# The down product of a feed-forward layer by one level of Strassen's scheme

## The chip, the cores and the metric

One core of a Trainium2 chip. Its engines are TensorE (PE, matmuls; PEld is its loading of the stationary operand), VectorE (DVE), ScalarE (ACT), GpSimd (POOL) and SyncE (SP, which here issues DMAs). The metric is the device time of one execution in microseconds, lower is better; the median of three runs is compared.

## The reference, cut to what matters

The program is one encoder block on 512 tokens of width 1024: a gated-delta branch and a short convolution, mixed, a layer norm, and then a feed-forward part, which is all that this change concerns:

```python
x = layer_norm(DEEPNORM_ALPHA * x + mixed @ w_out, ln1_g, ln1_b)
h = square(relu(x @ w_up + b_up))                    # 512 x 4096
x = layer_norm(DEEPNORM_ALPHA * x + h @ w_down + b_down, ln2_g, ln2_b)
```

`w_down` is 4096 x 1024, so the last product has 512 x 4096 x 1024 multiplications. Everything is float32.

## The kernel before

A float32 operand goes into TensorE as two parts, a higher part (`wh`, `hh`, rounded by a ScalarE copy) and a lower part (`wl`, `hl`, the VectorE difference of the operand and its higher part). One product of two tiles is then three matmuls: high x high, high x low, low x high. The helper `split` (lines 105 and 106) makes the two parts, `split_w` (lines 124 and 120) the same for the weights of `proj`.

After the first layer norm the product with `w_up` runs over 32 chunks of 128 columns. Each takes 24 matmuls of 128x512 in `proj` (lines 158 to 160); then `up_end` applies the ReLU on ScalarE (line 951) and squares on GpSimd (line 953), and the result `hf32[f]` (128 hidden units x 512 tokens, float32) stays in the slab under the tags A, A, D and C, eight chunks each.

The product with `w_down` is `tok_product` with `KF` = 32 chunks of rows. All eight banks of PSUM hold one accumulator each: four tiles of 128 tokens by two halves of 512 columns. Each chunk loads 512 KB of `w_down` over SP's queue (`load_w2`, line 890), splits it, splits `hf32[k]`, and for each of the eight accumulators runs `down`: three matmuls whose stationary operand is a 128x128 piece of the activations and whose moving operand is 512 columns of weights (line 899). The last four chunks (`tail`) are kept back and run tile after tile, so that a tile's end, `finish2`, runs beside the matmuls of the next tile. `finish2` adds the accumulators to `xs[t]`, the residual (line 993), takes the row statistics (`bn_stats`, line 873, and lines 877 to 880), and normalizes: the columns from `cut` on go through ScalarE (line 1002) and GpSimd (lines 1003 and 1004), the others through VectorE (lines 1008 and 1009). Then the tile is stored.

Weights pass through two rings: `raw` (three tiles in `wpool`) and `w2h`/`w2l` (four each in `ffn`). The split activations use the ring `wh`/`wl` of `wpool` (two each), which also holds the weights of the up product. Two pools matter for space: `late` holds the split input `x1` of the up product and is released at the very end.

Outside of regions marked `tc.manual_schedule` the framework orders instructions of an engine itself, by their dependences; inside such a region each engine listed keeps the order in which the program is written.

Of the kernel before, what the change touches and what calls it, by code (L numbers as in the profile page):

```python
# [61 lines left out]
def kernel(  # L62
# [912 lines left out]
    hpair = {}  # L975

    def h_split(k):
        if k % 2 == 0:
# [1 line left out]
        a, b = hpair[k - k % 2]  # L980
        a, b = a[:, k % 2, :], b[:, k % 2, :]
        split(a, b, hf32[k])
        return a, b

    def finish2(t, accs):
# [1 line left out]
        n = 2
        w = D // n
        part, end = row_stats(y, n, f"2_{t}")
        for j in range(n):  # L990
            js = slice(j * w, (j + 1) * w)
            o = j * w % NT
            tt(out=y[:, js], in0=y[:, js], in1=accs[j * w // NT][:, o:o + w], op=ALU.add)
# [74 lines left out]
```

## Time and profile before

| | |
|---|---|
| median of three runs | 1059.67 us (1056.95 to 1060.29) |
| the profiled execution | 1056.44 us, its span 1054.7 us |
| TensorE busy | 1025.2 us, 97% of the span |
| VectorE, ScalarE, GpSimd busy | 532.5, 452.6, 286.2 us |
| granted TensorE clock, mean | 0.991 |
| up product in `proj` | to 870.5 us |
| down product | 870.5 to 1044.9 us |
| HBM | 97.27 MB read |

Busy time of TensorE is modelled from pipelined instructions, so a matmul's row shows a longer duration than the distance between two of them. The rate comes from a stretch divided by its matmuls.

### The profile page before, as it was taken

How to read it: one execution, taken by the hardware profiler on the slowest of the kernel's cores; microseconds unless marked ns; L12 is line 12 of the kernel's file. 1: busy time of each engine (PE TensorE's matmuls, PEld its weight loads, DVE VectorE, ACT ScalarE, POOL GpSimd, SP SyncE). 2: the span in 40 equal slices, each digit the busy share in tenths (PEclk: the TensorE clock that was granted, in tenths of full speed). 3: DMA queues.
4: the chain of work that ended last, by engine and by line, in shares of the span. 5: the costliest groups of instructions: out<-in, count | busy, mean ns of one | idle time of the engine just before them, and what ended most of it. 6: DMA issues, size and time to landing. Idle time of an engine off the chain costs nothing.

```text
span 1054.7 us, 16601 instructions
## 1 busy us (share of the span) xinstructions
PE 1025.2 (97%) x6611; PEld 850.6 (81%) x6611; DVE 532.5 (50%) x923; ACT 452.6 (43%) x820; POOL 286.2 (27%) x527
## 2 busy tenths in 40 slices
PE   8898999999999999999999999989999999999996
PEld 5686888787888888888888888788888888888885
DVE  6675676767677775442322264761222243333346
ACT  5662556575757574353434232323333243232221
POOL 1051525252525346311130021263222220000005
PEclk9988999999999999999999999999999999999998
DMA  6413242323332222222335334222333342333312
GB/s 200 141 48 92 68 115 60 108 50 107 79 101 82 83 66 69 73 85 91 100 105 216 100 105 134 81 81 84 97 100 100 100 141 80 100 100 100 100 40 80
DMA packets 57094, 101.80 MB, mean 97 GB/s; under 512 B 30712, under 2 KB 32440, under 8 KB 57016
## 3 DMA queue, kind: packets, MB, share of 16 engines
q1 hardware_dynamic: 56584, 100.07, 31.2%
q8 instruction: 52, 0.85, 0.3%
q10 hardware_dynamic: 432, 0.66, 0.2%
q14 instruction: 26, 0.21, 0.1%
HBM read 97.27 MB, written 3.44 MB: 95 GB/s over the span
## 4 chain that ended last, share of the span: by engine, by line
PE 84%; DVE 6%; DMA 3%; POOL 3%; ACT 1%; issue 1%; SPq 1%; POOLq 0%; DVEq 0%; ACTq 0%
PE accd L899 16%; PE ps_in L158 11%; PE ps_in L160 10%; PE ps_in L159 10%; PE ps_up L159 5%; PE ps_up L160 5%; PE ps_up L158 5%; PE acco L899 3%; POOL X L550 2%; PE psup L946 1%; PE ps_osc L158 1%; PE ps_osc L160 1%; PE ps_osc L159 1%; PE ps_ogd L159 1%; PE ps_ogd L160 1%; PE ps_ogd L158 1%
## 5 line engine op out<-in xcount | busy, mean ns | idle before, releaser
L158 PE MATMUL ps_in<-xh,wh_in 128*128 128x512 f32 x576 | 238.5, 414 | 1.2 <-ACT wh_in L124 1.0
L160 PE MATMUL ps_in<-xh,wl_in 128*128 128x512 f32 x576 | 226.2, 393 | 1.8 <-DVE wl_in L120 1.8
L159 PE MATMUL ps_in<-xl,wh_in 128*128 128x512 f32 x576 | 225.8, 392 | 0.0
L120 DVE TENSOR_TENSOR wl_in<-raw_in,wh_in 128x1024 fp32r<-128x1024 f32 x70 | 97.4, 1391 | 86.9 <-ACT wh_in L124 86.3
L160 PEld LDWEIGHTS ps_in<-xh,wl_in 128*128 128x128 f32 x576 | 108.6, 189 | 26.8 <-DVE wl_in L120 2.7
L158 PEld LDWEIGHTS ps_in<-xh,wh_in 128*128 128x128 f32 x576 | 109.0, 189 | 21.8 <-ACT wh_in L124 2.0
L159 PEld LDWEIGHTS ps_in<-xl,wh_in 128*128 128x128 f32 x576 | 109.2, 190 | 17.7
L124 ACT ACTIVATE wh_in<-raw_in 128x1024 fp32r<-128x1024 f32 x70 | 73.9, 1056 | 71.0 <-PE ps_in L159 52.9
L899 PE MATMUL accd<-wh_down,hh 128*128 128x512 f32 x256 | 99.6, 390 | 0.0
L899 PE MATMUL accd<-wh_down,hl 128*128 128x512 f32 x256 | 99.4, 389 | 0.0
L899 PE MATMUL accd<-wl_down,hh 128*128 128x512 f32 x256 | 99.4, 389 | 0.0
L120 DVE TENSOR_TENSOR wl_up<-raw_up,wh_up 128x1024 fp32r<-128x1024 f32 x30 | 36.8, 1225 | 121.5 <-ACT wh_up L124 121.5
L158 PE MATMUL ps_up<-x1h,wh_up 128*128 128x512 f32 x224 | 87.1, 389 | 0.0
L159 PE MATMUL ps_up<-x1l,wh_up 128*128 128x512 f32 x224 | 87.1, 389 | 0.0
L160 PE MATMUL ps_up<-x1h,wl_up 128*128 128x512 f32 x224 | 87.1, 389 | 0.0
L953 POOL TENSOR_TENSOR hf<-r 128x512 f32<-128x512 f32 x32 | 46.3, 1447 | 118.6 <-ACT r L951 118.6
L124 ACT ACTIVATE wh_up<-raw_up 128x1024 fp32r<-128x1024 f32 x30 | 31.8, 1060 | 106.3 <-PE ps_up L159 98.7
L106 DVE TENSOR_TENSOR wl_down<-raw_down,wh_down 128x1024 fp32r<-128x1024 f32 x32 | 40.1, 1253 | 50.1 <-ACT wh_down L105 48.7
L899 PEld LDWEIGHTS accd<-wh_down,hh 128*128 128x128 f32 x256 | 48.0, 188 | 10.4 <-ACT wh_down L105 0.4
L899 PEld LDWEIGHTS accd<-wh_down,hl 128*128 128x128 f32 x256 | 48.0, 188 | 10.1
L899 PEld LDWEIGHTS accd<-wl_down,hh 128*128 128x128 f32 x256 | 48.0, 188 | 9.9
L105 ACT ACTIVATE wh_down<-raw_down 128x1024 fp32r<-128x1024 f32 x32 | 33.7, 1053 | 50.8 <-PE accd L899 50.2
(268 smaller groups left out, 1853.9 us busy)
## 6 DMA issues: line engine op xcount, KB each, us to landing
raw_in<-in_w_in SPq DMA_DIRECT2D x70, 512.0 KB, 3.6
raw_up<-in_w_up SPq DMA_DIRECT2D x32, 512.0 KB, 3.6
raw_down<-in_w_down SPq DMA_DIRECT2D x32, 512.0 KB, 3.5
grow<-gcd SPq DMA_DIRECT2D x8, 512.0 KB, 4.8
raw_osc<-in_w_o_sc SPq DMA_DIRECT2D x8, 512.0 KB, 3.6
raw_ogd<-in_w_o_gdn SPq DMA_DIRECT2D x8, 512.0 KB, 3.6
raw_out<-in_w_out SPq DMA_DIRECT2D x8, 512.0 KB, 3.6
xr<-in_xT SPq DMA_DIRECT2D x8, 256.0 KB, 5.0
```

Source lines behind the costliest of these rows:

```text
L105: act(out=hi, in_=src, func=AF.Copy)
L106: (lo_eng or nc.vector).tensor_tensor(out=lo, in0=src, in1=hi.bitcast(F32), op=ALU.subtract)
L120: (nc.gpsimd if pool else nc.vector).tensor_tensor(out=wl, in0=raw, in1=wh.bitcast(F32), op=ALU.subtract)
L124: act(out=wh, in_=raw, func=AF.Copy)
L158: nc.tensor.matmul(acc, wh[:, c], mh[k], start=(k == 0), stop=False)
L159: nc.tensor.matmul(acc, wh[:, c], ml[k], start=False, stop=False)
L160: nc.tensor.matmul(acc, wl[:, c], mh[k], start=False, stop=(k == KT - 1))
L550: sub(out=X[:, 0:r, k + 1:16], in0=X[:, 0:r, k + 1:16], in1=t[:, :, m], op=ALU.add)
L899: nc.tensor.matmul(acc[:, o], a[:, ts_], b[:, hs], start=start and j == 0, stop=stop and j == 2, skip_group_check=True)
L946: nc.tensor.matmul(acc[:, ts_], a[:, c], b[k][:, ts_], start=(k == 0 and t2 == 0 and j == 0), stop=(k == KT - 1 and t2 == 1 and j == 2), s ...
L953: nc.gpsimd.tensor_tensor(out=hfl, in0=r, in1=r, op=ALU.mult)
```

## The change

C = H W is computed by blocks. A pair of row chunks 2c and 2c+1 of `w_down` gives a 2 x 2 matrix of blocks on the right (rows 2c, rows 2c+1; left and right 512 columns), and the two chunks of the activations with the tokens 0 to 255 (`lo_t`) and 256 to 511 (`hi_t`) one on the left. One level of Strassen's scheme in Winograd's form takes seven products of blocks in place of eight, with sums and differences of blocks as operands. A product of blocks is, for each of two tiles of 128 tokens, three matmuls of 128x512 as before.

Seven accumulators and the added results do not fit into eight banks together, so the work runs in two passes over the 16 pairs, 32 steps in all. **Pass A** (steps 0 to 15) makes four products into aX, aY, aZ, aV (two banks each); at its last step (`left_over`) aX is copied to `e1` by ScalarE, and aY, aZ and aV are added to parts of `xs` by VectorE, six adds. **Pass B** (steps 16 to 31) goes on adding three products into aX, aZ and aY. It loads the weights again, 512 KB and 256 KB a step.

Sums of weights: in pass A GpSimd makes three differences of 128x512 in place in the raw weights (`sums_a`); in pass B one of 128x512, and one of 128x256 of the activations. Sums of activations in pass A: three of 128x256 on VectorE (two in `sums_a`, one in `parts_a`). All of these come before the splitting of their results by `split_d` and `split_h`. After pass A GpSimd also adds `e1` to parts of `xs`, one of six such adds in each of six steps.

Order: the loop is in a `manual_schedule` for all four engines. At step n it issues the loads of step n+3, the splits of step n+1, the sums of step n+2, and the matmuls of step n. Steps 0 and 1 are prepared, and step 2 is loaded, ahead of the loop. Raw weights go through a ring of seven tiles: three of `wpool`, two of `ffn`, two of the new pool `dn`, which takes the place of `late`, now released before the down product. The last five steps (`TAIL_B`) are all prepared after the loop's last matmuls have been issued, and then run for one half of the accumulators after the other: aY, aX, aZ for tokens of q = 0, then for q = 1, with the ends of two token tiles (`finish2`, now a generator) in between.

```diff
+ORDER = (2, 0, 3, 1)
+CUT = (0, NT, NT // 2, 3 * D // 4)
+TAIL_B = 5
+HOME_W, HOME_H = {11: "A", 15: "A"}, {11: "A", 15: "D"}
...
-    def h_split(k):
-        if k % 2 == 0:
-            hpair[k] = (wpool.tile([P, 2, NT], F32R, tag="wh", name=f"hh{k}"), wpool.tile([P, 2, NT], F32R, tag="wl", name=f"hl{k}"))
...
+    def load_d(k, lo, n, i):
+        j = i % 7
+        pool, tag, bufs = (wpool, "raw", 3) if j < 3 else (ffn, "rawx", 2) if j < 5 else (dn, "raw", 2)
+        raw = pool.tile([P, D], F32, tag=tag, name=f"raw_down{i}", bufs=bufs)
+        nc.sync.dma_start(out=raw[:, :n], in_=w_down[k][:, lo:lo + n])
+        return raw
+
+    def split_d(raw, n, i, home=None):
...
+        pool, tag = (ffn, "w2") if home is None else (home, "w1")
+        wh = pool.tile([P, n], F32R, tag=tag + "h", name=f"wh_down{i}", bufs=4)
+        wl = pool.tile([P, n], F32R, tag=tag + "l", name=f"wl_down{i}", bufs=4)
+        split(wh, wl, raw[:, :n])
+        return [(wh[:, j * NT:(j + 1) * NT], wl[:, j * NT:(j + 1) * NT]) for j in range(n // NT)]
+
+    late.release()
+    dn = tc.alloc_tile_pool(name="dn", bufs=1)
...
+    def split_h(k, parts, home=None):
...
+        pool, w, bufs = (dn, 3, 1) if i == 2 else (wpool, 4, 2)
+        sh_ = pool.tile([P, w, HT], F32R, tag="wh", name=f"hh{k}", bufs=bufs)
+        sl_ = pool.tile([P, w, HT], F32R, tag="wl", name=f"hl{k}", bufs=bufs)
+        o = 0
+        for src, w in parts:
+            split(flat(sh_[:, o:o + w]), flat(sl_[:, o:o + w]), src)
+            o += w
...
+    def sums_a(c, r0, r1):
+        sub = nc.gpsimd.tensor_tensor
+        sub(out=r0[:, right], in0=r0[:, right], in1=r0[:, left], op=ALU.subtract)
+        sub(out=r1[:, right], in0=r1[:, right], in1=r0[:, right], op=ALU.subtract)
+        sub(out=r1[:, left], in0=r1[:, left], in1=r1[:, right], op=ALU.subtract)
+        x, y = hf32[2 * c], hf32[2 * c + 1]
+        s = ffn.tile([P, 2, HT], F32, tag="S", name=f"sa{c}", bufs=2)
+        tt(out=s[:, 0], in0=x[:, hi_t], in1=y[:, hi_t], op=ALU.add)
+        tt(out=s[:, 1], in0=s[:, 0], in1=x[:, lo_t], op=ALU.subtract)
+        return r0, r1, s
+
+    def parts_a(c, r0, r1, s):
+        x, y = hf32[2 * c], hf32[2 * c + 1]
+        b11, t1 = split_d(r0, D, 2 * c)
+        a11, a22, s1, s2 = split_h(c, ((x[:, lo_t], 1), (y[:, hi_t], 1), (flat(s), 2)))
+        t4, t2 = split_d(r1, D, 2 * c + 1)
+        tt(out=y[:, hi_t], in0=y[:, lo_t], in1=s[:, 1], op=ALU.subtract)
+        return (a11, b11), (s2, t2), (s1, t1), (a22, t4)
+
+    def loads_b(c):
+        i = KF + 2 * c
+        return load_d(2 * c + 1, 0, D, i), load_d(2 * c, NT, NT, i + 1)
+
+    def sums_b(c, r0, r1):
+        nc.gpsimd.tensor_tensor(out=r1[:, :NT], in0=r0[:, NT:], in1=r1[:, :NT], op=ALU.subtract)
+        x = hf32[2 * c]
+        nc.gpsimd.tensor_tensor(out=x[:, lo_t], in0=x[:, lo_t], in1=x[:, hi_t], op=ALU.subtract)
+        return r0, r1
...
+    def weights_b(c, r0):
+        return split_d(r0, D, KF + 2 * c, HOME_W.get(c))
+
+    def sums_parts_b(c, r1):
+        a = split_h(KT + KF + c, ((hf32[2 * c + 1], 2), (hf32[2 * c][:, lo_t], 1)), HOME_H.get(c))
+        return a + split_d(r1, NT, KF + 2 * c + 1, HOME_W.get(c, dn))
+
+    def strassen(acc, a, b, q, start, stop):
+        qs = slice(q * P, (q + 1) * P)
+        for j, (l_, r_) in enumerate(((a[0], b[0]), (a[0], b[1]), (a[1], b[0]))):
+            nc.tensor.matmul(acc, l_[:, qs], r_, start=start and j == 0, stop=stop and j == 2, skip_group_check=True)
...
-    tok_product(KF, "d", h_split, lambda k: load_w2(w_down[k], f"down{k}"), finish2)
...
+    aX, aY, aZ, aV = ([ps(b, f"down{b}{i}_{q}") for q, b in enumerate(bs)] for i, bs in
+                  enumerate((("s", "s"), ("l", "o"), ("m", "g"), ("m", "g"))))
...
+    with tc.manual_schedule(engines=MANUAL):
+        for n in range(2 * KP - TAIL_B):
+            ahead(n + 3, 0)
+            if n:
+                ahead(n + 1, 2)
+            ahead(n + 2, 1)
...
+                for q in range(2):
+                    strassen(acc[q], a, b, q, n == 0, n == KP - 1 and acc is aV)
+                    if n == KP - 1:
+                        left_over(j, acc, q)
+            if n > KP and adds:
+                q, t, hs = adds.pop(0)
+                y = xs[t][:, hs]
+                nc.gpsimd.tensor_tensor(out=y, in0=y, in1=e1[q], op=ALU.add)
...
+        for i, n in enumerate(ends):
+            if i:
+                ahead(n, 1)
+            if i == 3:
+                weights(ends[0])
+            sums[n] = sums_parts_b(n - KP, got[n][1])
+        for n in ends[1:]:
+            weights(n)
+    last = list(zip(*(got[n] for n in range(2 * KP - TAIL_B, 2 * KP))))
+    with tc.manual_schedule(engines={mybir.EngineType.DVE, mybir.EngineType.PE}):
+        for q in (ORDER[1], ORDER[3]):
+            f1, f0 = finish2(q + 2), finish2(q)
+            next(f1), next(f0)
+            for acc, ab_ in ((aY, last[1]), (aX, last[0]), (aZ, last[2])):
+                for a, b in ab_:
+                    strassen(acc[q], a, b, q, False, b is ab_[-1][1])
+                if acc is aY:
+                    f1.send(acc[q]), f1.send(acc[q]), next(f1)
+                else:
+                    f0.send(acc[q])
+            next(f0)
...
```

## Rows read from the trace of the kernel before

**Rows 1.** The page: busy time by engine, and the chain that ended last.

```profile
PE 1025.2 (97%) x6611; PEld 850.6 (81%) x6611; DVE 532.5 (50%) x923; ACT 452.6 (43%) x820; POOL 286.2 (27%) x527
...
PE 84%; DVE 6%; DMA 3%; POOL 3%; ACT 1%; issue 1%; SPq 1%; POOLq 0%; DVEq 0%; ACTq 0%
PE accd L899 16%; PE ps_in L158 11%; PE ps_in L160 10%; PE ps_in L159 10%; PE ps_up L159 5%; PE ps_up L160 5%; PE ps_up L158 5%; PE acco L899 3%; POOL X L550 2%; PE psup L946 1%; PE ps_osc L158 1%; PE ps_osc L160 1%; PE ps_osc L159 1%; PE ps_ogd L159 1%; PE ps_ogd L160 1%; PE ps_ogd L158 1%
```

**Rows 2.** Busy time by stretches: the start, the down product, the tail.

```profile
core 0: us, PE busy (x) PEld busy (x) DVE busy (x) ACT busy (x) POOL busy (x), PEclk, DMA share, GB/s
0.00:10.00 10.00, 8.28 (x34) 5.98 (x34) 5.06 (x10) 6.53 (x10) 2.53 (x11) 1.00 0.80 273
...
870.50:1044.90 174.40, 174.40 (x769) 143.77 (x767) 67.98 (x81) 49.82 (x65) 10.63 (x5) 1.00 0.26 83
1044.90:1055.00 10.10, 0.04 (x1) 0.00 (x0) 5.21 (x12) 1.18 (x3) 4.18 (x4) 0.72 0.35 134
```

**Rows 3.** Groups by line and shape, from 840 us on: the down product's matmuls.

```profile
line engine op names shapes xcount | busy us, mean ns | idle before us <-releasers
L899 PE MATMUL accd<-wh_down,hh 128*128 128x512 f32 x256 | 99.6, 390 | 0.0
L899 PE MATMUL accd<-wh_down,hl 128*128 128x512 f32 x256 | 99.4, 389 | 0.0
L899 PE MATMUL accd<-wl_down,hh 128*128 128x512 f32 x256 | 99.4, 389 | 0.0
```

**Rows 4.** Groups by line and shape, several stretches: splits, squares, two-input operations.

```profile
L105 ACT ACTIVATE wh_down<-raw_down 128x1024 fp32r<-128x1024 f32 x32 | 33.7, 1053 | 50.8 <-PE accd L899 50.2 <-DMA raw_down<-in_w_down 0.6
L105 ACT ACTIVATE hh<-hf 128x512 fp32r<-128x512 f32 x32 | 18.7, 624 | 62.1 <-PE accd L899 58.2 <-PE ps_up L159 4.0
L953 POOL TENSOR_TENSOR hf<-r 128x512 f32<-128x512 f32 x7 | 9.6, 1372 | 27.6 <-ACT r L951 27.6
L120 DVE TENSOR_TENSOR wl_up<-raw_up,wh_up 128x1024 fp32r<-128x1024 f32 x5 | 6.1, 1226 | 19.1 <-ACT wh_up L124 19.1
...
L495 DVE TENSOR_TENSOR na<-pg,dec 128x256 f32<-128x256 f32 x8 | 2.8, 416 | 0.4 <-PE pg L491 0.4
...
L865 POOL TENSOR_TENSOR sga<-sga,yb 128x512 f32<-128x512 f32 x8 | 10.3, 1289 | 74.7 <-DVE sga L864 74.7
```

**Rows 5.** VectorE in order of time: start, duration, instructions one behind another.

```profile
871.08 0.69 DVE L106 TENSOR_TENSOR hl<-hf,hh 128x512 fp32r<-128x512 f32 x1 [2.15 <-ACT hh L105]
...
881.96 1.29 DVE L106 TENSOR_TENSOR hl<-hf,hh 128x512 fp32r<-128x512 f32 x2 [3.62 <-ACT hh L105]
...
401.07 1.42 DVE L495 TENSOR_TENSOR na<-pg,dec 128x256 f32<-128x256 f32 x4
```

**Rows 6.** In order of time: VectorE and GpSimd where they meet.

```profile
605.47 1.28 POOL L865 TENSOR_TENSOR sga<-sga,yb 128x512 f32<-128x512 f32 x1 [45.68 <-DVE sga L864]
605.50 2.33 DVE L120 TENSOR_TENSOR wl_ogd<-raw_ogd,wh_ogd 128x1024 fp32r<-128x1024 f32 x1 [0.18 <-ACT wh_ogd L124]
...
517.97 1.23 DVE L120 TENSOR_TENSOR wl_in<-raw_in,wh_in 128x1024 fp32r<-128x1024 f32 x1 [4.21 <-ACT wh_in L124]
...
518.50 1.84 POOL L835 TENSOR_TENSOR yb<-sgb,yb 128x512 f32<-128x512 f32 x1 [2.72 <-ACT sgb L834]
...
871.65 1.04 POOL L953 TENSOR_TENSOR hf<-r 128x512 f32<-128x512 f32 x1 [4.40 <-ACT r L951]
...
872.19 1.04 DVE L106 TENSOR_TENSOR hl<-hf,hh 128x512 fp32r<-128x512 f32 x1 [0.42 <-ACT hh L105]
```

**Rows 7.** In order of time: VectorE and GpSimd in the tail.

```profile
1041.12 2.40 POOL L1004 TENSOR_TENSOR xs<-xs,ln_b 128x1024 f32<-128x1024 f32 x1
1046.61 1.26 POOL L1004 TENSOR_TENSOR xs<-xs,ln_b 128x512 f32<-128x512 f32 x1
1050.91 0.72 POOL L1004 TENSOR_TENSOR xs<-xs,ln_b 128x256 f32<-128x256 f32 x1
...
1041.23 2.83 DVE L1008 SCALAR_TENSOR_TENSOR xs<-xs,mv,ln_g 128x512 f32<-128x512 f32 x1
...
1044.91 0.68 DVE L993 TENSOR_TENSOR xs<-xs,accd 128x512 f32<-128x512 f32 x1
1046.24 0.67 DVE L993 TENSOR_TENSOR xs<-xs,accd 128x512 f32<-128x512 f32 x1
```

**Rows 8.** DMA issues: size and median microseconds from issue to landing.

```profile
raw_down<-in_w_down SPq DMA_DIRECT2D x32, 512.0 KB, 3.5
```

**Rows 9.** TensorE's waits (in total, times, longest), and stretches as in rows 2.

```profile
PE pg L491 <- ACT qh L471: 2.3, 1, 2.3
PE pg L491 <- DVE ql L473: 2.3, 1, 2.3
...
PE px L571 <- DVE UT L564: 3.1, 1, 3.1
...
PE pt L932 <- DVE xs L926: 2.6, 2, 1.3
...
52.60:59.40 6.80, 5.30 (x22) 4.91 (x23) 6.36 (x14) 3.80 (x8) 0.36 (x1) 0.50 0.26 77
...
86.70:93.50 6.80, 6.12 (x167) 4.76 (x168) 2.75 (x12) 1.87 (x5) 0.00 (x0) 0.50 0.51 198
680.00:700.00 20.00, 17.23 (x111) 14.99 (x110) 19.89 (x23) 4.77 (x8) 14.05 (x5) 1.00 0.15 52
```

More of the change, by code (lines that the diff above doesn't have):

```diff
@@ L973 @@
     nc.sync.dma_start(out=lnc["b"], in_=ln2_b.partition_broadcast(P))
-    hpair = {}
-    def h_split(k):
-        if k % 2 == 0:
-            hpair[k] = (wpool.tile([P, 2, NT], F32R, tag="wh", name=f"hh{k}"), wpool.tile([P, 2, NT], F32R, tag="wl", name=f"hl{k}"))
[L980 to L985, printed above, removed]
-        y = xs[t]
[L987 to L993, printed above, removed]
+    def load_d(k, lo, n, i):
[4 more added lines that the diff above has]
+        return raw
@@ new lines, in split_d @@
+    def split_d(raw, n, i, home=None):
+        if isinstance(home, str):
+            ws = [[slab.tile([P, NT], F32R, tag=home, name=f"w{x}_down{i}_{j}", bufs=SLOTS[home]) for x in "hl"] for j in range(n // NT)]
+            for j, (wh, wl) in enumerate(ws):
+                split(wh, wl, raw[:, j * NT:(j + 1) * NT])
+            return [tuple(w) for w in ws]
+        pool, tag = (ffn, "w2") if home is None else (home, "w1")
[3 more added lines that the diff above has]
+        return [(wh[:, j * NT:(j + 1) * NT], wl[:, j * NT:(j + 1) * NT]) for j in range(n // NT)]
@@ new lines @@
+    late.release()
+    dn = tc.alloc_tile_pool(name="dn", bufs=1)
+    SLOTS = {"A": 16, "D": 8, "C": 8}
+    HT = NT // 2
+    lo_t, hi_t = slice(0, HT), slice(HT, NT)
+    three = [0]
+    def split_h(k, parts, home=None):
+        got = []
+        if home is not None:
+            for j, (src, w) in enumerate(parts):
+                if w == 1:
+                    t = slab.tile([P, 2, HT], F32R, tag=home, name=f"ha{k}", bufs=SLOTS[home])
+                    pair = t[:, 0:1], t[:, 1:2]
+                else:
+                    pair = [slab.tile([P, w, HT], F32R, tag=home, name=f"h{x}{k}", bufs=SLOTS[home]) for x in "hl"]
+                split(flat(pair[0]), flat(pair[1]), src)
+                got += [(pair[0][:, i], pair[1][:, i]) for i in range(w)]
+            return got
+        n = sum(w for _, w in parts)
+        i = three[0] % 3 if n == 3 else 0
+        three[0] += n == 3
+        pool, w, bufs = (dn, 3, 1) if i == 2 else (wpool, 4, 2)
[5 more added lines that the diff above has]
+            o += w
+        return [(sh_[:, j], sl_[:, j]) for j in range(o)]
@@ new lines, with flat, loads_a @@
+    left, right = slice(0, NT), slice(NT, D)
+    def flat(s):
+        return s.rearrange("p a t -> p (a t)")
+    def loads_a(c):
+        return load_d(2 * c, 0, D, 2 * c), load_d(2 * c + 1, 0, D, 2 * c + 1)
+    def sums_a(c, r0, r1):
[8 more added lines that the diff above has]
+        return r0, r1, s
@@ new lines, in sums_b, with parts_b @@
+    def sums_b(c, r0, r1):
[3 more added lines that the diff above has]
+        return r0, r1
+    def parts_b(c, r0, r1):
+        w, (a12, s4, s3, t3) = weights_b(c, r0), sums_parts_b(c, r1)
+        return (a12, w[0]), (s3, t3), (s4, w[1])
+    def weights_b(c, r0):
+        return split_d(r0, D, KF + 2 * c, HOME_W.get(c))
@@ new lines, in sums_parts_b, with finish2 @@
+    def sums_parts_b(c, r1):
[5 more added lines that the diff above has]
+            nc.tensor.matmul(acc, l_[:, qs], r_, start=start and j == 0, stop=stop and j == 2, skip_group_check=True)
+    def finish2(t):
+        y = xs[t]
+        n = ORDER.index(t)
+        part, end = row_stats(y, 2, f"2_{t}")
+        for j in range(2):
+            js = slice(j * NT, (j + 1) * NT)
+            tt(out=y[:, js], in0=y[:, js], in1=(yield), op=ALU.add)
@@ L994, in finish2 @@
             part(j)
+        yield
         mv, rs = end()
-        cut = (0, 0, NT, 3 * D // 4)[t]
+        cut = CUT[n]
         if cut < D:
@@ L1010, in finish2 @@
             (nc.sync if lo % NT else nc.scalar).dma_start(out=out[t][:, js], in_=y[:, js])
-    tok_product(KF, "d", h_split, lambda k: load_w2(w_down[k], f"down{k}"), finish2)
+        yield
+    KP = KF // 2
+    aX, aY, aZ, aV = ([ps(b, f"down{b}{i}_{q}") for q, b in enumerate(bs)] for i, bs in
+                  enumerate((("s", "s"), ("l", "o"), ("m", "g"), ("m", "g"))))
+    steps = [(loads_a, sums_a, parts_a, c) for c in range(KP)] + [(loads_b, sums_b, parts_b, c) for c in range(KP)]
+    e1, got = [None, None], {}
@@ new lines, in ahead, with left_over, weights @@
+    def ahead(n, what):
+        if n < 2 * KP:
+            c = steps[n][3]
+            got[n] = steps[n][what](c, *got.get(n, ()))
+    def left_over(n, acc, q):
+        if n == 0:
+            e1[q] = slab.tile([P, NT], F32, tag="zt", name=f"e1{q}", bufs=2)
+            act(out=e1[q], in_=acc[q], func=AF.Copy)
+        else:
+            y = xs[(q, q + 2, q + 2)[n - 1]][:, (right, right, left)[n - 1]]
+            tt(out=y, in0=y, in1=acc[q], op=ALU.add)
+    def weights(n):
+        w, (a12, s4, s3, t3) = weights_b(n - KP, got[n][0]), sums[n]
+        got[n] = (a12, w[0]), (s3, t3), (s4, w[1])
@@ new lines @@
+    adds = [(q, t, hs) for q in range(2) for t, hs in ((q + 2, left), (q + 2, right), (q, right))]
+    for n in range(2):
+        for what in range(3):
+            ahead(n, what)
+    ahead(2, 0)
+    with tc.manual_schedule(engines=MANUAL):
[4 more added lines that the diff above has]
+            ahead(n + 2, 1)
+            c = steps[n][3]
+            for j, (acc, (a, b)) in enumerate(zip((aX, aY, aZ, aV) if n < KP else (aX, aZ, aY), got[n] if n < KP else [got[n][i] for i in (0, 2, 1)])):
+                for q in range(2):
[6 more added lines that the diff above has]
+                nc.gpsimd.tensor_tensor(out=y, in0=y, in1=e1[q], op=ALU.add)
+        ends = list(range(2 * KP - TAIL_B + 1, 2 * KP))
+        for n in ends[2:]:
+            ahead(n, 0)
+        sums = {}
+        for i, n in enumerate(ends):
[6 more added lines that the diff above has]
+            weights(n)
@@ new lines @@
+    last = list(zip(*(got[n] for n in range(2 * KP - TAIL_B, 2 * KP))))
[8 more added lines that the diff above has]
+                    f1.send(acc[q]), f1.send(acc[q]), next(f1)
+                else:
+                    f0.send(acc[q])
+            next(f0)
@@ L1013 @@
     ffn.tile([P, PAD_RIGHT // 4], F32, tag="pad", name="pad_right", bufs=1)
-    late.release()
+    dn.release()
 def _layout(x, w_in, conv_qkv, a_log, dt_bias, gdn_norm_w, w_o_gdn, conv_sc, w_o_sc, w_out,
```

## The prediction

> **What bounds the kernel now.** I read the page from the top. TensorE is busy in 97% of the span and carries 84% of the chain that ended last, the down product alone 16% [rows 1]. The table by stretches then shows that from 870.5 us, where the up product ends, to 1044.9 us TensorE is never idle, at the full granted clock, while VectorE works 68 of 174.4 us, ScalarE 50 and GpSimd 11 [rows 2]. This stretch is what the change rebuilds. Its groups give the price of a matmul: 768 matmuls (three lines of 256) in 174.4 us are 0.227 us each; the 389 ns of a row are a modelled end in a pipeline [rows 3]. After the last matmul comes a tail of VectorE, ScalarE, GpSimd and one store, 9.8 us.
>
> The sum is made against the profiled execution: span 1054.7 us, 1056.4 us in all, 0.3% below the median of 1059.67 us. Some 0.3% is also what a measurement of this kernel can tell from no change.
>
> **Matmuls.** A step is one pair of row chunks. Pass A has 4 products of 2 x 3 matmuls (24, 5.45 us), pass B has 3 (18, 4.09 us); 16 steps of each are 672 matmuls in place of 768. Removed: 96 x 0.227 = 21.8 us. Were TensorE still the bound, the kernel would be that much faster. So the question is whether the operands arrive in time.
>
> **Preparation of a pass A step.** VectorE: two 128x1024 lower halves (1.226 us), one 128x512 (0.69 [rows 5]), and five 256-wide (two lower halves, the three sums `s`, `s`, `y`), for which the nearest row is 128x256 at 0.416 [rows 4]. One behind another they take less than their durations, since starts overlap: two of 512 took 1.29 us together, so 0.60 for the second; four of 256 took 1.42 us, so 0.335 each [rows 5]; by the same 0.09 us, 1.14 for 1024. VectorE alone: 2 x 1.14 + 0.60 + 5 x 0.335 = 4.56 us, which fits into 5.45. ScalarE: 2 x 1.053 + 0.624 + two of 256 at most 0.62 each, 4.0 us, fits. GpSimd: three chained subtractions of 128x512 with two different inputs, 1.29 us each undisturbed [rows 4], 3.9 us, fits too. Each engine by itself hides under TensorE.
>
> **But VectorE and GpSimd do not run beside each other here.** The lower half `wl_ogd` starts 0.03 us after GpSimd's `sga` and takes 2.33 us in place of 1.226: it ends 1.08 us after GpSimd does. The other way round GpSimd's `yb` starts half a microsecond into a lower half and takes 1.84 us in place of 1.29, ending 1.14 us after VectorE; `hl`, behind GpSimd's square, takes 1.04 in place of 0.69 [rows 6]. Whoever comes second waits for the other's instruction, and only some 0.15 us of its fixed part is hidden. The exception is VectorE's adds with one input in PSUM: `xs<-xs,accd` kept 0.67 us beside GpSimd [rows 7]. All operands of the lower halves and sums lie in SBUF, so all of them count.
>
> The two engines therefore share one account. In pass A GpSimd's three take 3 x 1.14 = 3.43 us, VectorE's eight 4.56, less 0.06 for each of the three that follow GpSimd (1.08 against 1.14): 4.38. Together **7.81 us a step, against 5.45 of TensorE**. In pass B: VectorE 1.14 + 2 x 0.60 + 0.335 less 2 x 0.06, 2.56; GpSimd one subtraction of 512 (1.14) and one of 256 (0.72 [rows 7] less 0.15, 0.57); together 4.28 against 4.09. Bounds for a pass A step: whole durations with nothing hidden, 2 x 1.226 + 0.69 + 5 x 0.416 + 3 x 1.29 = 9.1 (and 5.0 in pass B); below, GpSimd's subtractions at 0.90, as its square (1.04 undisturbed) would pay: 7.1. I take 7.81, because a 512-wide GpSimd operation with two inputs stands in the rows.
>
> The Trainium skill (SBUF — State Buffer, section Who interferes with whom) has this as an exclusive lock: a VectorE instruction with two SBUF inputs and a GpSimd instruction that reads SBUF exclude each other, and the second is blocked until the first is done. Taken as whole instructions this rule would make an estimated 9.1 us a step and some 30 us more in all than my sum; the rows agree on the lock but show 0.15 us of each instruction outside it, so I keep the lower figure.
>
> **The lookahead does not absorb this.** Only steps 0 and 1 are prepared ahead of the hand-ordered loop; buffers (two steps of weights, seven raw tiles) let the rest run some two steps in front. The up product's stretch has room for these two: per chunk of 5.45 us VectorE's one lower half takes 1.23 and GpSimd's one square 1.4 [rows 4].
>
> **The sum, from 870.5 us on.** (a) The split of step 1's activations, whose buffers are up's weights, 0.60 + 2 x 0.335 = 1.27, and the square of chunk 31, 0.90: 2.2. (b) Raw tiles 5 and 6 lie in the pool that takes the place of x1, so they load only when up is over: 3.5 us to landing [rows 8], then step 2's two last subtractions; some of that is filled with other work. Nothing to 5, I take 3.0. (c) Steps 2 to 15: 14 x 7.81 = 109.3. (d) Between the passes VectorE adds six accumulators to `xs` (0.68 each, one input in PSUM) and queues step 17's splits behind them: 0 to 4.1, I take 2.0, as GpSimd goes on meanwhile. (e) 16 x 4.28 = 68.5. (f) GpSimd's six adds of `e1`, 6 x 1.08 = 6.5. (g) When the last weight is split, TensorE still has 3 + 15 + 45 matmuls (the rest of aX, aZ, the second half): 63 x 0.227 = 14.3. Together 205.8 in place of 174.4: **+31.4**.
>
> (h) The tail. In the last tile both halves were added behind 1044.9, at 1044.91 and 1046.24, because VectorE came late: its `xs` of 1041.23 took 2.83 us beside GpSimd's 2.40 [rows 7]. Now the left half is added while aZ runs, 3.4 us earlier, which takes one add and one statistic, 1.3 us, off the path; 0 to -1.3, I take -1.3. Loads: 1 MB per 7.81 us (134 GB/s), then 0.79 MB per 4.28 us (184 GB/s), 64 issues on SP in place of 32; the first stretch moved 273 GB/s [rows 2]. I cost them at nothing; their cover is three steps of lookahead, and one late load would cost at most its 3.5 us. Sum: 1056.4 + 31.4 - 1.3 = **1086.5 us**, said as 1087.
>
> **Rivals.** *Faster: the account never fills.* If GpSimd's subtractions fitted into the gaps that VectorE leaves (waits for ScalarE, the fixed parts of its short operations), TensorE stays the bound: 1056.4 - 21.8 - 1.3 + 0 to 3 = 1033 to 1036, say 1034. For it speak the three single loads, all under 5.45, against it every pair that meets in [rows 6]. It decides by one number: everything but (c) is 96.5 us, so the change breaks even at a pass A step of (174.4 + 1.3 - 96.5) / 14 = 5.7 us. To get there from 7.81, two of three subtractions would have to cost nothing. I give it 0.19. In between, within 0.3%, lies little: 0.05.
>
> *Slower still: the clock.* In pass A TensorE would work 5.45 of 7.81 us, with waits in each step: for the second weight tile, whose lower half stands last in VectorE's order. In the kernel before, after two waits of 2.3 us near 50 us, the granted clock was 0.5 (1.2 of 2.4 GHz) from 52.6 to 59.4 us, and after a wait of 3.1 us again from 86.7 for 6.8 us; with two waits of 1.3 us between 680 and 700 us it stayed at 1.00 [rows 9]. Mine are 2.4 us a step in all, longer where GpSimd runs ahead and takes every second turn. At half the clock a step needs 10.9 us of TensorE, so each fall of 6.8 us costs up to 3.4 us. Four falls give up to 13.6: 1087 to 1101. Chance 0.16.
>
> **How the numbers follow.** The forecast has 0.60, the clock 0.16, faster 0.19, the same 0.05. The forecast's own range is 1072 (7.1 a step, 14 x 0.7 = 10, and nothing for b and d, 5) to 1100 (half of what the whole durations would add, 14 x 1.3 + 16 x 0.75 = 30). With the clock on top the upper end is 1110, and the lower end goes down to 1064 for a lock partly filled; the faster rival stays outside. Slower by over 0.3% 0.76, within 0.3% 0.05, faster 0.19.
>
> **What would show it.** Right: in the down stretch TensorE's idle time ends on VectorE's lower halves; VectorE and GpSimd together are busy all the time, with instructions of 128x1024 around 2.3 us and subtractions around 1.8 to 2.5; pass A takes some 115 us and pass B with its end some 90. Wrong: pass A near 87 us with TensorE busy throughout, VectorE's lower halves at 1.23 us beside GpSimd's subtractions. A granted clock under 1.00 after 870 us is the second rival. The first idle time of TensorE should come at step 2 or 3, not before 880 us.

## The result, and the profile after

The changed kernel takes 1093.86 us (median of four runs, 1093.1 to 1095.0), the kernel before 1059.98 beside it: ratio 1.0325, interval 1.0300 to 1.0349, slower by 34 us. The forecast was 1087. The profiled execution takes 1093.1 us, its span is 1091.4.

The page, lines that answer to [rows 1]:

```profile
PE 1024.9 (94%) x6515; PEld 834.6 (76%) x6515; DVE 667.7 (61%) x1061; ACT 493.2 (45%) x904; POOL 416.4 (38%) x613
...
PE 70%; DVE 16%; issue 4%; DMA 4%; POOL 3%; ACT 2%; SPq 0%; POOLq 0%; DVEq 0%; ACTq 0%
```

VectorE's share of the chain rises from 6% to 16% and TensorE's falls from 84% to 70%, though TensorE's busy time is that of before: 96 matmuls fewer, the others with longer modelled durations. So busy time shows nothing of the saving here, and the stretches have to be read, as in [rows 2]:

```profile
core 0: us, PE busy (x) PEld busy (x) DVE busy (x) ACT busy (x) POOL busy (x), PEclk, DMA share, GB/s
871.00:894.00 23.00, 18.43 (x75) 13.47 (x73) 19.05 (x21) 11.23 (x19) 15.64 (x11) 1.00 0.43 137
894.00:904.30 10.30, 7.03 (x16) 5.05 (x17) 10.27 (x8) 0.29 (x1) 9.99 (x8) 0.50 0.32 102
936.00:975.20 39.20, 31.22 (x122) 21.76 (x121) 39.03 (x41) 14.65 (x25) 23.34 (x15) 1.00 0.42 134
994.70:1054.00 59.30, 49.85 (x203) 36.87 (x201) 59.30 (x55) 30.07 (x52) 44.04 (x30) 1.00 0.50 156
1054.00:1080.80 26.80, 23.62 (x86) 17.55 (x86) 24.52 (x39) 9.25 (x16) 10.75 (x6) 0.87 0.13 49
1080.80:1091.40 10.60, 0.12 (x1) 0.00 (x0) 7.17 (x13) 1.58 (x3) 5.38 (x4) 0.71 0.27 100
```

The down product lasts from 871.0 to 1080.8 us, 209.7 against 174.4 before. In the even middle of pass A (936.0 to 975.2, five steps of 7.84 us) VectorE is busy for 39.0 of 39.2 us, GpSimd for 23.3; in pass B VectorE has not a gap. What TensorE waits for, 871 to 1081 us (in total, times, longest):

```profile
PEld downl L1092 <- DVE wl_down L113: 26.8, 20, 3.7
PE downl L1092 <- DVE wl_down L113: 17.9, 15, 3.3
PEld downs L1092 <- DVE hl L113: 14.2, 14, 1.2
```

These are VectorE's lower halves (L113 after the change). One step in order of time, first VectorE, then GpSimd, then TensorE's two matmuls that waited (start, duration, in brackets the wait before):

```profile
936.60 1.83 DVE L113 TENSOR_TENSOR hl<-hf,hh 128x256 fp32r<-128x256 f32 x2
938.36 0.68 DVE L113 TENSOR_TENSOR hl<-sa,hh 128x512 fp32r<-128x512 f32 x1
938.96 1.21 DVE L113 TENSOR_TENSOR wl_down<-raw_down,wh_down 128x1024 fp32r<-128x1024 f32 x1
940.09 0.41 DVE L1064 TENSOR_TENSOR hf<-hf,sa 128x256 f32<-128x256 f32 x1
940.43 0.41 DVE L1054 TENSOR_TENSOR sa<-hf,hf 128x256 f32<-128x256 f32 x1
940.88 1.40 DVE L1055 TENSOR_TENSOR sa<-sa,hf 128x256 f32<-128x256 f32 x1
942.20 2.31 DVE L113 TENSOR_TENSOR wl_down<-raw_down,wh_down 128x1024 fp32r<-128x1024 f32 x1
...
936.03 1.78 POOL L1049 TENSOR_TENSOR raw_down<-raw_down 128x512 f32<-128x512 f32 x1 [0.43 <-DMA raw_down<-in_w_down]
940.46 1.54 POOL L1050 TENSOR_TENSOR raw_down<-raw_down,raw_down 128x512 f32<-128x512 f32 x1 [2.64 <-DMA raw_down<-in_w_down]
942.08 1.36 POOL L1051 TENSOR_TENSOR raw_down<-raw_down 128x512 f32<-128x512 f32 x1
...
938.15 0.50 PE L1092 MATMUL downs<-wh_down,hl 128*128 128x512 f32 x1 [0.92 <-DVE hl L113]
940.23 0.49 PE L1092 MATMUL downl<-wl_down,hh 128*128 128x512 f32 x1 [0.63 <-DVE wl_down L113]
```

Read the durations as waits. A lower half of 1024 takes 1.21 us with GpSimd idle and 2.31 where a difference (L1051) starts just before it; two of 256 take 1.83 in place of 0.75 beside L1049. In these rows an instruction that is too long for its shape stood still, and its neighbour on the other engine is what it stood for.

### The profile page after: what moved, and what is told of

Same layout as the page of the kernel before. It is cut to its first block, busy times and chain, and to the rows that moved or that the text cites. A ratio compares the mean times of both kernels' runs of the same rounds, so it can differ in the third digit from the quotient of the medians.

```text
span 1091.4 us, 16896 instructions
## 1 busy us (share of the span) xinstructions
PE 1024.9 (94%) x6515; PEld 834.6 (76%) x6515; DVE 667.7 (61%) x1061; ACT 493.2 (45%) x904; POOL 416.4 (38%) x613
## 4 chain that ended last, share of the span: by engine, by line
PE 70%; DVE 16%; issue 4%; DMA 4%; POOL 3%; ACT 2%; SPq 0%; POOLq 0%; DVEq 0%; ACTq 0%
PE ps_in L165 12%; PE ps_in L167 11%; PE ps_in L166 11%; DVE hl L113 4%; DVE wl_down L113 4%; PE ps_up L165 4%; PE ps_up L166 4%; PE ps_up L167 4%; PE acco L906 3%; DMA raw_down<-in_w_down 2%; PE psup L953 1%; PE ps_osc L165 1%; PE ps_osc L167 1%; PE ps_ogd L165 1%; PE ps_ogd L166 1%
## 5 line engine op out<-in xcount | busy, mean ns | idle before, releaser
L113 DVE TENSOR_TENSOR wl_down<-raw_down,wh_down 128x1024 fp32r<-128x1024 f32 (+1 forms) x66 | 91.6, 1404 | 10.2 <-ACT wh_down L112 10.0
L131 ACT ACTIVATE wh_up<-raw_up 128x1024 fp32r<-128x1024 f32 x30 | 31.8, 1060 | 105.5 <-PE ps_up L166 97.9
L112 ACT ACTIVATE wh_down<-raw_down 128x1024 fp32r<-128x1024 f32 (+1 forms) x66 | 57.9, 916 | 15.3 <-POOL raw_down L1051 9.0
L113 DVE TENSOR_TENSOR hl<-hf,hh 128x256 fp32r<-128x256 f32 (+1 forms) x62 | 56.7, 952 | 0.0
L487 POOL TENSOR_TENSOR grow<-grow,y 128x1024 f32<-128x1024 f32 x8 | 20.1, 2515 | 83.9 <-ACT y L387 45.0
L167 PEld LDWEIGHTS ps_up<-x1h,wl_up 128*128 128x128 f32 x224 | 42.0, 188 | 8.8
L165 PEld LDWEIGHTS ps_up<-x1h,wh_up 128*128 128x128 f32 x224 | 42.0, 188 | 8.7
L166 PEld LDWEIGHTS ps_up<-x1l,wh_up 128*128 128x128 f32 x224 | 42.0, 188 | 8.6
L557 POOL TENSOR_TENSOR X<-X,xt 128x26 f32<-128x26 f32 (+7 forms) x128 | 40.9, 320 | 10.0
```

Of the source, the lines that this page charges most:

```text
L131: act(out=wh, in_=raw, func=AF.Copy)
L165: nc.tensor.matmul(acc, wh[:, c], mh[k], start=(k == 0), stop=False)
L166: nc.tensor.matmul(acc, wh[:, c], ml[k], start=False, stop=False)
L167: nc.tensor.matmul(acc, wl[:, c], mh[k], start=False, stop=(k == KT - 1))
L487: nc.gpsimd.tensor_tensor(out=qd, in0=qd, in1=qk[:, 1, :].rearrange("p (c t) -> p c t", t=P).unsqueeze(1).broadcast_to([P, 2, NCH, P]), op ...
L557: sub(out=X[:, 0:r, k + 1:16], in0=X[:, 0:r, k + 1:16], in1=t[:, :, m], op=ALU.add)
```

## The experiments

Theory: VectorE's instructions with two inputs in SBUF and GpSimd's differences exclude each other, so the two engines share one account, which sets the pace. Rivals: TensorE's clock or the waits by themselves; too many loads; the new order and its buffers; any GpSimd work in those places, whatever it reads. `e1`, `e3` and `e4` are single executions; the other runs are medians of four to twelve.

**Without GpSimd's differences.** `e1_no_sums` leaves out all five of a pair, so the products are made of other operands.

```diff
-        sub(out=r0[:, right], in0=r0[:, right], in1=r0[:, left], op=ALU.subtract)
...
-        nc.gpsimd.tensor_tensor(out=x[:, lo_t], in0=x[:, lo_t], in1=x[:, hi_t], op=ALU.subtract)
```

> The three GpSimd subtractions of pass A and the two of pass B are left out; everything else stands. Shared account (VectorE and GpSimd exclude each other): pass A falls to TensorE's 5.45 us a step, pass B to 4.09, VectorE's lower halves return to 1.23 us; 672 x 0.227 = 152.6 us of matmuls plus 1 to 4 us at the start in place of 209.7, so 1036 to 1041 us. Late operands for another reason (loads, the ring of raw tiles, buffers): TensorE goes on waiting, over 1060 us.

1042.14 us, 1 us above the range. Loads, order, buffers and matmuls are unchanged, and all 16 steps of pass A take 5.44 us, those of pass B 4.08 but for two; VectorE's lower halves of 1024 are back at 1.22 us. So loads and order cost 5.4 us at most, which is what the down product takes here above its matmuls, and the change without these sums is faster than before by 1.5% (before 1057.94 here). The differences themselves are the cost.

**Fills in their place.** `e3_fills_for_sums` has GpSimd write zeros into the same columns, at the same places, in place of the sums.

```diff
-        sub(out=r0[:, right], in0=r0[:, right], in1=r0[:, left], op=ALU.subtract)
...
+        for half in (r0[:, right], r1[:, right], r1[:, left]):
+            nc.gpsimd.memset(half, 0.0)
```

> Each of the five GpSimd subtractions is a GpSimd memset of the same columns, so GpSimd writes and does not read; order, buffers and dependences stay. Shared account by GpSimd's reading: VectorE's lower halves stay at 1.23 us beside the memsets, pass A is TensorE's or near it, 1036 to 1048 us. Exclusion by anything that GpSimd does: like the kernel after, less only what a memset is shorter, 1065 to 1095 us. A chain (GpSimd, then ScalarE, then VectorE) that is too long: over 1065 us as well, but with short lower halves.

1039.07 us, pass A at 5.44. VectorE, then GpSimd, in order of time:

```profile
911.55 1.22 DVE L113 TENSOR_TENSOR wl_down<-raw_down,wh_down 128x1024 fp32r<-128x1024 f32 x1
...
914.58 1.23 DVE L113 TENSOR_TENSOR wl_down<-raw_down,wh_down 128x1024 fp32r<-128x1024 f32 x1 [0.68 <-ACT wh_down L112]
...
911.68 0.53 POOL L1050 MEMSET raw_down<- 128x512 f32 x1 [1.97 <-DVE hl L113]
914.21 1.00 POOL L1050 MEMSET raw_down<- 128x512 f32 x2 [1.99 <-DMA raw_down<-in_w_down]
```

The fill at 911.68 lies wholly inside a lower half; it keeps its 0.53 us and the lower half its 1.22. So GpSimd's waiting for the same buffers, holding them and writing them is harmless; what is left of the differences is their reading. The Trainium skill (SBUF — State Buffer, section Who interferes with whom) says the same: a two-input VectorE instruction contends with a GpSimd instruction that reads SBUF, not with one that only writes it. Here the runs agree.

**One more difference.** `e4_one_more_sum` makes the third difference of each pair of pass A twice, so its operand is another one.

```diff
         sub(out=r1[:, left], in0=r1[:, left], in1=r1[:, right], op=ALU.subtract)
+        sub(out=r1[:, left], in0=r1[:, left], in1=r1[:, right], op=ALU.subtract)
```

> A fourth GpSimd subtraction in each pass A step (the third one made twice). Shared account: 14 to 16 times 1.14 us, 16 to 18 us more, 1109 to 1112 us, pass A steps of 9.0 us. If the account does not bind, GpSimd, busy 130 of 210 us, takes it into its idle time: 1093 to 1096 us.

1110.24 us, 16.4 above the changed kernel; by the two traces the down product is 16.9 us longer, and TensorE's steps 2 to 15 take 9.03 us on average. Fourteen pairs at the account's 1.14 us give 16.0: next to nothing of the added instruction hides, though GpSimd had been idle for 40% of an even step of the changed kernel. The granted clock was 0.50 in six stretches of pass A here, in two of the changed kernel, and the sum still holds: TensorE was not what the steps waited for.

**The sums on VectorE.** `e2_sums_on_vector` also moved a helper's subtraction of the same name in an early stage, and so spoils its total; `e5_vector_clean` repeats it for the down product alone.

```diff
-        sub = nc.gpsimd.tensor_tensor
+        sub = tt
...
-        nc.gpsimd.tensor_tensor(out=r1[:, :NT], in0=r0[:, NT:], in1=r1[:, :NT], op=ALU.subtract)
+        tt(out=r1[:, :NT], in0=r0[:, NT:], in1=r1[:, :NT], op=ALU.subtract)
```

> The same five subtractions a pair, but on VectorE. Shared account: a subtraction costs VectorE 0.60 us in place of 1.14 of the account, so a pass A step takes 4.56 + 3 x 0.60 = 6.4 us and pass B 3.6 us, under TensorE's 4.09; 2.2 + 3 + 14 x 6.36 + 4.1 + 16 x 4.09 = 164 us in place of 209.7, so about 1047 us (1043 to 1057). VectorE simply overloaded (203 of 210 us busy, so every instruction moved onto it adds its time): 48 x 0.69 + 16 x 1.1 = 50 us more, about 1140 us.

> The five subtractions a pair on VectorE, and nothing else touched: the edit of e2_sums_on_vector had also moved a helper of the same name in the first branch, and the up product there ended at 918.6 us in place of 871. Shared account: the down product as it was there, 183.7 us with pass A steps of 6.73, behind an up product that ends at 871: 871 + 184 + 12 = 1067 us (1062 to 1072), between before and after. If VectorE's overload alone decides, whatever GpSimd does, the time is that of after or more: 1094 us and over.

`e2`: 1114.22 us, ratio 1.0525 (1.0490 to 1.0560). It missed by 67 us. The up product ended at 918.6 us in place of 871, which is 48 of them; the down product took 183.7 where 164 was expected, with steps of 6.73 in place of 6.4 (5 us in all) and three long ones after the change of passes (5.56, 6.90 and 8.95, some 9 us). `e5`: 1067.51 us, ratio 1.0090 (1.0057 to 1.0122), with 183.0 for the down product and 6.73 for a step of pass A, as expected. VectorE has each sum at 0.69 us where GpSimd's cost the pair 1.14:

```profile
943.07 0.68 DVE L1049 TENSOR_TENSOR raw_down<-raw_down 128x512 f32<-128x512 f32 x1
943.78 0.69 DVE L1050 TENSOR_TENSOR raw_down<-raw_down,raw_down 128x512 f32<-128x512 f32 x1
944.51 0.69 DVE L1051 TENSOR_TENSOR raw_down<-raw_down 128x512 f32<-128x512 f32 x1
```

Moving work from an engine with 40% of idle time onto one without a gap makes the kernel 26 us faster: in the profile's sense GpSimd was idle, but not in VectorE's account. Starts show that a chained sum comes 0.72 us after the last, 0.12 more than an independent one.

**The sums by DMA.** With signs changed (so that every weight sum is an addition) an accumulating DMA can make them, and neither engine reads.

```diff
+    def plus(out, in_):
+        nc.gpsimd.dma_start(out=out, in_=in_, accum_op=ALU.add)
...
-        sub(out=r0[:, right], in0=r0[:, right], in1=r0[:, left], op=ALU.subtract)
+        plus(r0[:, right], r0[:, left])
```

`e6_sums_by_dma` gives all four of a pair to the DMA and the activations' difference of pass B to VectorE; `e7_half_by_dma` leaves two chained ones of pass A to the DMA, the rest to VectorE.

> The weight sums are made by accumulating DMAs within SBUF (three of 256 KB a pass A step, one in pass B), with signs arranged so that all are additions; neither VectorE nor GpSimd computes them, the activations' difference of pass B goes to VectorE. Shared account: VectorE alone needs 4.56 us a step, TensorE is the bound again, 1040 to 1048 us, below before. Transfers as the new bound: 1.75 MB a pass A step are 320 GB/s at 5.45 us, more than any stretch so far moved (273); if they manage 200 to 270 GB/s a step takes 6.5 to 8.7 us, 1055 to 1090 us.

> As e6_sums_by_dma, but the first sum of a pass A step and the one of pass B are made on VectorE (4.56 + 0.65 = 5.2 us a step, 3.6 in pass B), two accumulating DMAs stay. Shared account: still under TensorE's 5.45 us, 1040 to 1050 us, with 1.5 MB a step (280 GB/s). If the transfers bind, better than e6_sums_by_dma by a fifth of the loss; if VectorE waits in order for raw tiles, pass A steps of 6 us or more, over 1050 us.

1145.67 us, ratio 1.0819 (1.0789 to 1.0849), and 1154.32, ratio 1.0905 (1.0879 to 1.0931): both missed by far. `e6`, its waits of 871 to 1140 us, then a DMA issue row (size, median from issue to landing):

```profile
ACT wh_down L112 <- DMA raw_down<-raw_down: 130.5, 33, 9.0
POOL raw_down L1044 <- DMA raw_down<-raw_down: 129.5, 28, 6.3
...
raw_down<-raw_down POOLq DMA_DIRECT2D x64, 256.0 KB, 5.2
```

One addition lands 5.2 us after its issue; the three of a pair depend on each other, and GpSimd waits for a landing twice a step (28 waits, 129.5 us), so a step of pass A takes 12.0 us on average from the fourth on. I had counted bandwidth and not the chain's latency. What the account says of VectorE did hold (its lower halves are at 1.22 us beside the DMAs). `e7` has one addition fewer in the chain and steps as long, 11 to 15 us from the third on: the sum that VectorE makes for the next pair stands in its order behind the lower half that needs the last landing, and GpSimd waits for VectorE before it issues again (11 waits, 86.1 us between 880 and 1060).

**Less work on VectorE.** `e8_less_vector_one_dma` keeps one DMA addition a pair (a single one can be issued early), puts the others on VectorE, takes the first activation difference into the up product on GpSimd, and splits unsummed activations 512 wide. `e9_less_vector` is the same with no DMA.

```diff
+        if f % 2:
+            nc.gpsimd.tensor_tensor(out=x[:, NT // 2:], in0=hfl[:, NT // 2:], in1=x[:, NT // 2:], op=ALU.subtract)
...
+        nc.gpsimd.dma_start(out=r0[:, right], in_=r0[:, left], accum_op=ALU.add)
```

> VectorE's account is cut under TensorE's: the activations' first sum is made on GpSimd during the up product, the second in place, the third and fourth in pass B; one weight sum a step comes from an accumulating DMA issued with the loads, three steps ahead; the two others and the adds of e1 stay on VectorE; aV is added in pass B. Pass A: 2 x 1.14 + 0.60 + 4 x 0.335 + 2 x 0.65 less one 0.335 = 5.2 us, pass B 3.3, both under 5.45 and 4.09. Shared account: TensorE bound, 1040 to 1047 us. If the DMA's latency (4.5 us for the load and 5.2 for the accumulation) does not fit into three steps: pass A steps over 6 us, over 1052 us.

> As e8_less_vector_one_dma without any accumulating DMA: all weight sums on VectorE. Pass A 5.83 us, pass B 3.9 us: 14 x 0.38 = 5.3 us over TensorE's 152.6, 3 to 6 us more around the change of passes and at the end: 1046 to 1054 us. If a sum on VectorE costs 0.72 each, as the chained ones did, 1050 to 1057.

1059.57 us, ratio 1.0019 (1.0008 to 1.0031), and 1077.19, ratio 1.0182 (1.0164 to 1.0200); missed by 12 us and 23. By instruction counts VectorE needs less than 5.45 us in `e8`, but a step took 5.89. ScalarE, which makes the higher halves in a fixed order, now comes late, as a row of ScalarE at the start of `e8` and two of VectorE in a step of `e9` show:

```profile
875.02 1.06 ACT L112 ACTIVATE wh_down<-raw_down 128x1024 fp32r<-128x1024 f32 x1 [6.53 <-DMA raw_down<-raw_down]
```

```profile
941.42 1.23 DVE L113 TENSOR_TENSOR wl_down<-raw_down,wh_down 128x1024 fp32r<-128x1024 f32 x1 [0.54 <-ACT wh_down L112]
...
945.57 1.22 DVE L113 TENSOR_TENSOR wl_down<-raw_down,wh_down 128x1024 fp32r<-128x1024 f32 x1 [0.59 <-ACT wh_down L112]
```

An engine that is nearly full has no room for a wait: 0.54 and 0.59 us a step in `e9`, whose steps take 7.25 us in place of 5.83, are lost time at once.

**A version that beats both.** `e10_one_dma_reordered` mends `e8` where its trace shows waits: the DMA's sum is on VectorE for the first three pairs of pass A and the last five of pass B, and in pass A the fourth sum moves a step forward and the splits are put in an order in which VectorE needn't wait.

```diff
+        if c > 2:
+            nc.gpsimd.dma_start(out=r0[:, right], in_=r0[:, left], accum_op=ALU.add)
...
+        tt(out=r1[:, left], in0=r1[:, left], in1=r1[:, right], op=ALU.add)
...
+        act(out=w[1][0], in_=r1, func=AF.Copy)
+        act(out=sh_[:, 3], in_=x[:, lo_t], func=AF.Copy)
```

> This is the kernel with no GpSimd arithmetic on the weights and one DMA-added sum a pair (1059.57 us), mended at the three places where its own trace shows TensorE waiting. (1) The sum that the DMA adds is made on VectorE for the first three pairs of pass A: there step 0 took 10.5 us in place of 5.44, since the DMA's sum for step 1 landed late and ScalarE waited in order; expected 5.5 to 7, so -4. (2) The fourth weight sum moves a step forward, and VectorE takes its lower halves in an order that leaves no wait for ScalarE: a pass A step took 5.89 us with 0.59 of VectorE waiting in it; VectorE's work is 2 x 1.14 + 3 x 0.60 + 3 x 0.335 = 5.1 us, so TensorE's 5.45 should be the bound again; 13 steps x 0.45 = -6. (3) For the last five pairs of pass B the sum is made on VectorE: the first group of the tail took 13.0 us there in place of some 3.4 to 8; -5. If waits were the cause, in those places: 1043 to 1048 us, 1.0 to 1.5% faster than before, pass A steps of 5.44 to 5.5 and pass B at 4.08. Rival: VectorE at 5.1 of 5.45 us has no slack for the irregular order of arrivals, so that other waits take their place: pass A steps of 5.7 or more and 1053 us or more. Bound from the kernels without sums or with fills in their place: 1039 to 1042.

1049.75 us against 1058.11, ratio 0.9920 (0.9905 to 0.9935): faster than before by 0.8%, though not in the range expected. Pass A, pass B up to the last five steps, and those steps:

```profile
871.00:959.40 88.40, 87.90 (x387) 72.09 (x386) 83.54 (x129) 52.77 (x82) 16.16 (x18) 1.00 0.85 230
959.40:1004.20 44.80, 44.80 (x199) 37.14 (x198) 44.16 (x78) 26.47 (x45) 6.88 (x8) 1.00 0.89 239
1004.20:1037.80 33.60, 26.88 (x91) 18.78 (x90) 29.21 (x56) 13.38 (x22) 8.28 (x5) 0.80 0.17 59
```

TensorE has no wait in pass B, and in pass A all steps but one (6.61) take 5.44. Points 1 and 2 held. Point 3 was wrong: the first group of the last five steps took 14.7 us, where `e8` had 13.0 and `e1` 5.9. VectorE is full in pass B (44.16 of 44.80 us, in `e8` 45.33 of 45.70), so it can have prepared little ahead, and the sums that I moved onto it come on top. This is read from the busy time and not shown by a run; up to 8 us may still lie in that place.

## Why the prediction came out

The forecast held in direction and size: +37 us by the two profiled executions (1093.1 less 1056.4) against +30.1. Term by term, with the ends of preparation read from VectorE's order after the change:

| term | forecast | measured | read as |
|---|---|---|---|
| (a) rest of steps 0 and 1 | 2.2 | 7.7 | 870.5 to 879.0, less 0.84 for two sums of step 2 |
| (b), (c) start wait, 14 steps | 112.3 | 112.7 | 879.0 to 990.9, with those 0.84 |
| (d), (e), (f) pass B | 77.0 | 75.3 | to the end of the last weight's lower half, 1066.18 |
| (g) 63 matmuls | 14.3 | 14.6 | to 1080.76 |
| (h) tail | -1.3 | +0.8 | 1080.76 to 1091.4, against 9.8 |

**The account (c)** is right. The even steps take 7.80 to 7.89 us, as computed (7.81), VectorE or GpSimd is busy for 208.2 of the 209.9 us, and `e1`, `e3`, `e4` and `e5` change one side of it at a time with the result that it gives. GpSimd's difference at the price of the square (7.1) is too low. The rule of the Trainium skill taken as whole instructions (SBUF — State Buffer, section Who interferes with whom; an estimated 9.1 us a step) is too dear: the measurement decides for 7.8. In pass B the steps without GpSimd's adds take 4.31 us (4.28 forecast). Of the signs that the prediction named, pass A was to take some 115 us and pass B with its end some 90; by the table they took 120.4 and 89.9, and most of the difference is (a). By line, VectorE and GpSimd, 871 to 1081 us (count, busy, mean ns):

```profile
L113 DVE TENSOR_TENSOR wl_down<-raw_down,wh_down 128x1024 fp32r<-128x1024 f32 x43 | 71.2, 1658 | 4.1 <-ACT wh_down L112 4.1
L1055 DVE TENSOR_TENSOR sa<-sa,hf 128x256 f32<-128x256 f32 x14 | 16.7, 1191 | 0.5
...
L1049 POOL TENSOR_TENSOR raw_down<-raw_down 128x512 f32<-128x512 f32 x13 | 21.8, 1675 | 6.6 <-DMA raw_down<-in_w_down 6.6
L1050 POOL TENSOR_TENSOR raw_down<-raw_down,raw_down 128x512 f32<-128x512 f32 x14 | 21.2, 1515 | 27.9 <-DMA raw_down<-in_w_down 27.6
```

Mean durations are too long by the waits on either side. They were forecast as 2.3 and 1.8 to 2.5 us; the means are 1.66 and 1.5 to 1.7, since by no means all pairs meet. The sum of the account didn't depend on who waits for whom.

**(a) was mis-sized, by 5.5 us, most of the error.** I read from the code that only step 1's activations were left over. In fact the splits of both steps' activations and one lower half of 1024 came behind the up product, with two squares on GpSimd. VectorE at the start, with one row of GpSimd ahead:

```profile
869.95 2.15 POOL L1051 TENSOR_TENSOR raw_down<-raw_down 128x512 f32<-128x512 f32 x1
...
870.87 2.68 DVE L113 TENSOR_TENSOR hl<-hf,hh 128x256 fp32r<-128x256 f32 x2
873.48 0.68 DVE L113 TENSOR_TENSOR hl<-sa,hh 128x512 fp32r<-128x512 f32 x1
874.08 0.41 DVE L1064 TENSOR_TENSOR hf<-hf,sa 128x256 f32<-128x256 f32 x1
874.42 2.06 DVE L113 TENSOR_TENSOR wl_down<-raw_down,wh_down 128x1024 fp32r<-128x1024 f32 x1
...
885.26 1.23 DVE L113 TENSOR_TENSOR wl_down<-raw_down,wh_down 128x1024 fp32r<-128x1024 f32 x1 [3.85 <-ACT wh_down L112]
```

By the forecast's own prices these are 2 x 1.27 + 2 x 0.335 + 1.14 + 2 x 0.90 = 6.15 us. GpSimd's last difference of step 1 (the first row, 1.14 in the account) and the end of the lower half before it, 0.4, make up the rest of the 7.7. For that reason TensorE's first wait, 0.79 us, ended at 872.4 and did not come after 880. What held ScalarE's copies back were the two weight copies before them, which had waited 3.2 and 2.5 us for GpSimd's differences; GpSimd in turn had waited 2.7 and 1.3 us for loads, which SP issued only as buffers of raw weights came free (by its waits, behind VectorE's `wl_up` and GpSimd's L1050).

The last row is (b): VectorE stands for 3.85 us while GpSimd makes three differences. The size is near the 3.0 forecast, but by luck, for the load came late for another reason. The chain followed back, and GpSimd:

```profile
876.88 4.47 DMA raw_down<-in_w_down
...
881.48 1.28 POOL L1050 TENSOR_TENSOR raw_down<-raw_down,raw_down 128x512 f32<-128x512 f32 x1 [6.09 <-DMA raw_down<-in_w_down]
```

This load did not go out when the up product ended, at 871. In SP's order it stood behind one issued at 876.50, whose buffer VectorE's lower half of 874.42 had freed at 876.48. So it landed at 881.35 and not near 874.5, and the lateness of (a) made that of (b).

**(h) had the wrong sign.** aX was complete at 1077.4 us and aZ 3.4 us later, as said, but VectorE was not there to add. Two rows of VectorE, one of GpSimd:

```profile
1072.98 2.33 DVE L1110 SCALAR_TENSOR_TENSOR nmr<-mv,rs 128x1 f32<-128x1 f32 x1
1081.26 0.68 DVE L1101 TENSOR_TENSOR xs<-xs,downs 128x512 f32<-128x512 f32 x1
...
1072.90 2.40 POOL L1113 TENSOR_TENSOR xs<-xs,ln_b 128x1024 f32<-128x1024 f32 x1
```

A one-column instruction with two inputs in SBUF, started 0.08 us behind GpSimd's normalization, stood for 2.33 us, and what came after it had no gap in which to catch up. The left half was added at 1081.26, behind the last matmul, not beside aZ. I had used this lock in the sum of the steps and left it out of the tail, with the row that shows it before my eyes [rows 7].

**The second rival's clock falls came**, and cost next to nothing. The granted clock was 0.50 (1.2 of 2.4 GHz) for 10.2 us from 894.1 on, after a wait of 2.10 us and within the next one, and for three stretches of 3.4 us, 20.4 in all before 1065; through the even steps, with two waits in each (0.92 and 0.63 us in the step shown), it stayed at 1.00 (the third row of the stretches). Between 885 and 905 us GpSimd had all its loads and took every second turn, so that VectorE's lower halves took 2.28 to 2.31 us and one step 15.29. But the steps (b) and (c) still come to 112.7 us in all: from 885.26 us to the end of pass A VectorE has no gap, so at half the clock a step's TensorE work still lay beside the account, and GpSimd's lead was paid back in later steps. The price that I gave the falls assumed that TensorE would be what the step waits for.

**The faster rival** is what `e1` shows: with an account that never fills the time is 1042, not 1034. Its down product takes 158.0 us, 5.4 more than 174.4 less the 21.8 of the matmuls: two steps after the change of passes are long (4.90 and 6.39 in place of 4.08) while GpSimd's six adds of the tile `e1` take turns with VectorE (958.9 to 969.4 us), and the first group of the last five steps takes 5.9 in place of 3.4. Its tail is 11.1 us where 8.5 was forecast. The run `e3`, where those two steps are not long, is 3.1 us faster.

## What to carry to other kernels

Before work is put on an idle GpSimd, add its two-input instructions to VectorE's, less some 0.15 us each, and compare that sum, not either engine's busy time, with the engine that should stay the bound. A saving of matmuls is worth only as much as the engine that prepares their operands has room for: here 21.8 us of TensorE were bought with 3.4 us a step of an account that was full. When moving work to another place, count the chain's latency and the order on the engine that feeds the full one: `e6` and `e9` lost more by these than they took off.
